# The three low-rank inputs of an RWKV-7 time-mix: shifting the input, or mixing the weights

## The chip, the cores and the metric

One core of one Trainium2 chip runs the whole program. The metric is the device time of one execution in microseconds (us). The engines are TensorE (PE; PEld is its weight load), VectorE (DVE), ScalarE (ACT), GpSimd (POOL) and SyncE (SP), which issues nearly all the transfers.

## What is computed

The program is a decoder trunk of two layers for 1024 tokens of 1024 channels, float32: an RWKV-7 time-mix with its MLP, then sliding-window attention with its MLP. The change is in the time-mix, in the inputs of its projections:

```python
xx = token_shift(h) - h                    # token_shift: the row before, zeros ahead of the first
xs = h[None] + xx[None] * mu[:, None, None, :]
r, k, v = jnp.einsum('nbtc,ncd->nbtd', xs[:3], w_rkv)
xv, xw, xa, xg = xs[2], xs[3], xs[4], xs[5]
w_log = -jax.nn.softplus(-(w0 + jnp.tanh(xw @ w1) @ w2)) - 0.5
a = jax.nn.sigmoid(a0 + (xa @ a1) @ a2)
g = jax.nn.sigmoid(xg @ g1) @ g2
```

Six inputs are made from h and its shifted copy. Three feed full matrices (r, k, v: 1024 x 1024), three feed low-rank ones: decay (w1, 64 columns), rate (a1, 64) and gate (g1, 160). Then come a recurrence over the tokens for 16 heads, a normalisation, the gate and an output matrix.

## The kernel before

**Precision.** A float32 product is made of three products in float32r: each operand is split into a high half (a cast on ScalarE, line 129) and a low half (a subtraction, line 130), and `mm3` adds high x high, high x low and low x high (lines 134 to 136). So every operand costs a cast and a subtraction ahead of PE. Weights arrive in a "wr" tile (5 buffers), are split into "wh" (4) and "wl" (3), and split inputs lie in "m2k" tiles (24 buffers). A few small products use plain float32, such as line 535, the sums of squares per head.

**Parts.** The projections run in three parts of 256, 256 and 512 tokens (`PARTS`), each a call of `project`. `channels` normalises and transposes x into h: tiles "b8" of 257 columns, with the token ahead in column 0. `steps` makes the differences of neighbouring tokens on GpSimd for the parts of 256. `shifted` makes one input i: for each of 8 tiles of 128 channels it mixes h and its neighbour with mu (line 353; lines 357 and 358 in the part of 512) and splits the result, on GpSimd's subtraction for the first 8, 4 and 0 tiles of a part (`POOLED`), else on VectorE's. `thin` multiplies such an input with a low-rank matrix; `lora_out` and `gate_out` are the second, wide product of the low-rank pairs. `values` makes v for a part, in one PSUM bank per 128 tokens, and `prod` one 128-channel group of r or k. The pools hold eight PSUM banks: four "big" for the projections and the MLP, two "sm" and two "sq" for the recurrence.

**Order.** In a part, the gate's second product of the part before (`left`) and the first thin input alternate for nine steps; then values; then the groups of r and k, after each of which a number of steps of the generator `small` is taken (`STEPS1`, `STEPS2`): the rest of the thin inputs, their second products, and the channels of the next part. Results go to HBM (dP, dG, dV). A part's groups of heads end with the inverse norms of k (lines 548 to 560): line 559 closes a group, and the recurrence reads its result in `prep` (600 to 602).

**The recurrence** takes units of 128 tokens and 8 heads, 16 in all, through `prep`, `inner`, `solve` (on GpSimd), `join`, `chunks` and `finish`. Its instructions have priority over the projections. Units 0 to 3 need part 0, units 4 to 7 part 1, units 8 to 15 part 2. After unit 7 the first half of the tokens goes on: `mixed` and `mix_out`, then the MLP of that half, beside units 8 to 15. A scheduler puts the instructions into an order for each engine by priority and by its own estimate of time when the program is built; every engine, and SP's queue of transfers, then works in that order.

## Time and profile before

| | |
|---|---|
| median of 3 runs | 2687.38 us (2681.1 to 2687.82) |
| profiled execution | 2683.85 us, its span 2682.1 us |
| mean granted clock of TensorE | 0.974 of full speed |
| busy: PE, PEld, DVE, ACT, POOL | 2549.6, 2066.2, 1688.0, 1289.1, 616.9 us |
| instructions: PE, DVE, ACT, POOL | 15226, 3204, 2670, 1213 |
| DMA | 349.62 MB, mean 130 GB/s |

The profile shows one execution. Busy time is the union of an engine's instructions; matmuls overlap each other, so the sum of their durations is more than PE's busy time. A granted clock of 1 is TensorE at 2.4 GHz, 0.5 at 1.2 GHz, and a mean lies between. A wait names the instruction that came last before the waiting one could start. The projections fill the first 666 us, the recurrence runs from 104 to about 1230 us, the MLPs and the attention from about 770 us to the end.

### The profile page before, as it was taken

The page shows a single profiled execution, that of the slowest core. Times are in us where ns is not written, and L with a number is a line of the kernel's source. Part 1 is how long each engine was busy: PE and PEld are TensorE (multiplying, and loading weights), DVE is VectorE, ACT ScalarE, POOL GpSimd, SP SyncE. Part 2 cuts the span into 40 slices and gives each one's busy share as a digit, 9 for nine tenths or more (in the row PEclk, how much of TensorE's full clock was granted, in tenths as well). Part 3 has the DMA queues.
Part 4 walks back from the last instruction along what each step waited for, and adds up shares of the span by engine and source line. Part 5 has one row for each costly group of instructions (what it writes and reads, how often), then busy time and mean ns, then how long its engine had stood idle before and what let it go on. Part 6 is the DMA issues. An engine that isn't in the chain of part 4 may idle for free.

```text
span 2682.1 us, 43180 instructions
## 1 busy us (share of the span) xinstructions
PE 2549.6 (95%) x15226; PEld 2066.2 (77%) x15226; DVE 1688.0 (63%) x3204; ACT 1289.1 (48%) x2670; POOL 616.9 (23%) x1213
## 2 busy tenths in 40 slices
PE   7978988998889999999999999999999999999999
PEld 5867766765767777778888888888888888888887
DVE  8678788665766666545467876445899544444444
ACT  5555566455444434334455555334666433434342
POOL 6276643741464444410010000001000000000000
PEclk9988989999889999999999999999999999999999
DMA  5756644654634444333434444342446332423332
GB/s 178 203 171 171 181 115 121 181 145 148 178 101 117 121 117 117 109 103 119 142 94 150 123 129 146 92 154 90 136 142 204 114 102 91 125 91 102 98 98 96
DMA packets 440633, 349.62 MB, mean 130 GB/s; under 512 B 97105, under 2 KB 360417, under 8 KB 440417
## 3 DMA queue, kind: packets, MB, share of 16 engines
q1 hardware_dynamic: 423008, 344.77, 42.5%
q10 hardware_dynamic: 17408, 2.10, 0.5%
q8 instruction: 120, 1.97, 0.3%
q14 instruction: 97, 0.79, 0.1%
HBM read 280.71 MB, written 57.67 MB: 126 GB/s over the span
## 4 chain that ended last, share of the span: by engine, by line
PE 54%; DVE 2%; DMA 0%; ACT 0%; issue 0%; POOL 0%; DVEq 0%; ACTq 0%; POOLq 0%
PE big L134 17%; PE big L135 17%; PE big L136 17%; PE sm L134 1%; PE sm L135 0%; PE sm L136 0%; PE sq L956 0%; PE sq L957 0%; PE big L252 0%; DVE sc L962 0%; DVE wl L130 0%; DVE m2k L260 0%; PE sq L933 0%; DMA wr<-in_b_wq 0%; DVE b L1038 0%; DVE st L966 0%
## 5 line engine op out<-in xcount | busy, mean ns | idle before, releaser
L129 ACT CAST wh<-wr 128x512 fp32r<-128x512 f32 x741 | 458.2, 620 | 872.4 <-PE big L136 457.5
L130 DVE TENSOR_TENSOR wl<-wr,wh 128x512 fp32r<-128x512 f32 x741 | 529.4, 718 | 485.5 <-issue 226.0
L135 PE MATMUL big<-wl,m2k 128*128 128x512 f32 (+1 forms) x1472 | 580.6, 395 | 7.2 <-DVE wl L130 5.4
L134 PE MATMUL big<-m2k,wh 128*128 128x512 f32 (+3 forms) x1528 | 576.4, 380 | 9.8 <-ACT m2k L129 4.8
L136 PE MATMUL big<-m2k,wl 128*128 128x512 f32 (+2 forms) x1528 | 571.3, 376 | 7.4 <-DVE wl L130 7.3
L135 PE MATMUL big<-m2k,wh 128*128 128x512 f32 (+2 forms) x1528 | 571.1, 375 | 7.3 <-POOL m2k L130 4.2
L136 PE MATMUL big<-wh,m2k 128*128 128x512 f32 (+1 forms) x1472 | 567.5, 392 | 2.8 <-POOL m2k L130 2.8
L134 PE MATMUL big<-wh,m2k 128*128 128x512 f32 (+1 forms) x1472 | 515.9, 395 | 9.8 <-ACT m2k L129 7.5
L134 PEld LDWEIGHTS big<-m2k,wh 128*128 128x128 f32 (+1 forms) x1528 | 290.3, 190 | 70.8 <-ACT m2k L129 6.9
L136 PEld LDWEIGHTS big<-m2k,wl 128*128 128x128 f32 (+1 forms) x1528 | 290.8, 191 | 59.6 <-DVE wl L130 10.1
L134 PEld LDWEIGHTS big<-wh,m2k 128*128 128x128 f32 x1472 | 281.3, 192 | 71.1 <-ACT m2k L129 9.2
L135 PEld LDWEIGHTS big<-m2k,wh 128*128 128x128 f32 (+1 forms) x1528 | 290.6, 190 | 58.5 <-POOL m2k L130 6.7
L135 PEld LDWEIGHTS big<-wl,m2k 128*128 128x128 f32 x1472 | 282.1, 192 | 69.2 <-DVE wl L130 10.4
L136 PEld LDWEIGHTS big<-wh,m2k 128*128 128x128 f32 x1472 | 281.2, 191 | 59.3 <-POOL m2k L130 3.3
L680 POOL TENSOR_TENSOR tmp<-Xs,TT 128x60 f32<-128x60 f32 (+24 forms) x496 | 193.6, 390 | 142.0 <-DMA Xs<-dXs 105.4
L130 DVE TENSOR_TENSOR m2k<-relu,m2k 128x512 fp32r<-128x512 f32 (+1 forms) x200 | 137.0, 687 | 122.7 <-ACT m2k L129 122.0
L682 POOL TENSOR_TENSOR TT<-TT,tmp 128x60 f32<-128x60 f32 (+24 forms) x496 | 199.1, 401 | 37.8
L129 ACT CAST m2k<-relu 128x512 fp32r<-128x512 f32 (+1 forms) x272 | 146.4, 544 | 46.3 <-DVE relu L353 33.8
L322 DVE TENSOR_TENSOR b<-b,big 128x512 f32<-128x512 f32 x192 | 124.8, 681 | 10.2 <-PE big L136 9.7
L223 POOL TENSOR_TENSOR ss<-ss,mhalf 128x4 f32<-128x4 f32 (+1 forms) x10 | 8.9, 888 | 488.7 <-DVE ss L222 488.7
L223 POOL TENSOR_TENSOR qn<-qn,mhalf 128x8 f32<-128x8 f32 x16 | 26.7, 1671 | 399.3 <-DVE qn L222 346.0
L314 ACT ACTIVATE relu<-relu 128x512 f32<-128x512 f32 x128 | 80.8, 632 | 3.5
(229 smaller groups left out, 3089.7 us busy)
## 6 DMA issues: line engine op xcount, KB each, us to landing
wr<-in_mlp_w SPq DMA_DIRECT2D x512, 256.0 KB, 2.7
wr<-in_a_w_rkv SPq DMA_DIRECT2D x144, 256.0 KB, 3.1
ld<-dP SPq DMA_DIRECT2D x16, 1024.0 KB, 7.7
dS<-sc SPq DMA_DIRECT2D x28, 512.0 KB, 2.9
row<-dS SPq DMA_DIRECT2D x112, 128.0 KB, 2.8
dP<-stg SPq DMA_DIRECT2D x64, 128.0 KB, 2.8
AR<-RA SPq DMA_DIRECT2D x32, 256.0 KB, 4.5
Xs<-dXs SPq DMA_DIRECT2D x64, 128.0 KB, 2.7
```

The lines of the kernel that those rows point to most:

```text
L129: self.nc.scalar.copy(hi, src)
L130: (engine or self.nc.vector).tensor_tensor(lo, src, hi.bitcast(F32), ALU.subtract)
L134: mm(ps, ah, bh, start=start, stop=False)
L135: mm(ps, ah, bl, start=False, stop=False)
L136: mm(ps, al, bh, start=False, stop=stop)
L223: nc.gpsimd.tensor_tensor(dst, dst, self.mhalf[:, :n], ALU.pow)
L314: nc.scalar.activation(r, r, AF.Square)
L322: nc.vector.tensor_tensor(v, v, ps[tt], ALU.add)
L680: nc.gpsimd.tensor_tensor(v, Xs[:, k:k + 1, k + 1:].broadcast_to([P, m, n]), TT[:, 0:m, k:k + 1].broadcast_to([P, m, n]), ALU.mult)
L682: nc.gpsimd.tensor_tensor(TT[:, 0:m, k + 1:], TT[:, 0:m, k + 1:], v, ALU.add)
```

## The change

The token shift is linear, so h + (shifted - h) * mu times W equals h times ((1 - mu) W) plus the shifted h times (mu W). The three low-rank matrices (64 + 64 + 160 = 288 columns) are multiplied by (1 - mu) and by mu once, in part 0, by GpSimd; 256 of the mixed columns are split into halves and stored to HBM (dL), and read back in parts 1 and 2. h itself is split once, 257 columns of it, and each pair of tiles is streamed twice through PE, the second time moved by one column (`small_in`). The last 32 columns of the gate are kept in plain float32 (`last`): their products are written to four groups of 32 PSUM partitions, two of the eight channel tiles in each, and `gate_in` adds the four. All three inputs' first products are now done in the nine steps ahead of values; three PSUM banks are held meanwhile. "m2k" tiles become 516 columns wide, and the step counts are shorter.

```diff
--- before.py
+++ after.py
@@ -41,6 +41,9 @@
 PARTS = [(0, 256), (256, 256), (512, 512)]
 PART = [(i, t) for i, (_, n) in enumerate(PARTS) for t in range(0, n, TB)]
 
+MIXED = [(3, 0, 2), (4, 2, 2), (5, 4, 5)]
+UNITS = 9
+
 M2K = 24
 WR = 5
 WH = 4
@@ -55,8 +58,8 @@
 ORDER2 = 'cispfj'
 POOLED = (8, 4, 0)
 
-STEPS1 = (0, 2, 2, 2, 2, 2, 2, 2, 2, 3, 3, 3, 3, 4, 4, 4)
-STEPS2 = (2, 2, 2, 2, 2, 2, 2, 3, 3, 3, 3, 3, 3, 3, 3, 3)
+STEPS1 = (0, 1, 1, 1, 1, 1, 1, 1, 1, 1, 1, 2, 2, 2, 2, 2)
+STEPS2 = (1, 1, 1, 1, 1, 2, 2, 2, 2, 2, 2, 2, 2, 2, 2, 2)
 
 PACE0 = 0.6
 PACE1 = 1
@@ -111,7 +114,10 @@
         return self.sq.tile([P, 512], F32, tag="sq", name=self.nm("sq"))
 
     def m2k(self):
-        return self.t(self.mp, "m2k", [P, 512], F32R, M2K)
+        return self.m2k_wide()[:, :512]
+
+    def m2k_wide(self):
+        return self.t(self.mp, "m2k", [P, 516], F32R, M2K)
 
     def parts(self, n):
 
@@ -204,6 +210,11 @@
                                     channel_multiplier=0)
         self.mhalf = cp.tile([P, NT * H], F32, name="mhalf")
         nc.vector.memset(self.mhalf, -0.5)
+
+        self.mixes = cp.tile([P, KT, 2, UNITS], F32, name="mixes")
+        for i, u0, n in MIXED:
+            for j, v in enumerate((self.vec2[:, i * KT:(i + 1) * KT], self.vec[:, m0 + i * KT:m0 + (i + 1) * KT])):
+                nc.vector.tensor_copy(self.mixes[:, :, j, u0:u0 + n], v.unsqueeze(2).broadcast_to([P, KT, n]))
         self.hlast = cp.tile([P, KT], F32, name="hlast")
         nc.vector.memset(self.hlast, 0.0)
 
@@ -330,6 +341,8 @@
         self.dP = [part(f"dP{g}_", lambda m: [P, 4, GP, m]) for g in range(NG)]
         self.dG = [part(f"dG{g}_", lambda m: [P, GP, m]) for g in range(NG)]
         self.dV = part("dV", lambda m: [m, C])
+        self.dL = [d(f"dL{k}", [2, P, 512]) for k in range(KT)]
+        self.dL3 = d("dL3", [P, KT, 2, 32])
         self.dZ = [d(f"dZ{i}", [P, KT, TH]) for i in range(2)]
         self.dX = [d(f"dX{i}", [TH, C]) for i in range(2)]
 
@@ -360,17 +373,67 @@
             self.split(hi, lo, a, nc.gpsimd if k < POOLED[self.pt] else None)
             yield hi, lo
 
-    def thin(self, hT, i, n, W, outs):
-
-        w = W.shape[-1]
-        m = min(512 // w, KT)
-        for k, (xh, xl) in enumerate(self.shifted(hT, i, n)):
-            if k % m == 0:
-                wh, wl = self.weight(W[k * P:min(k + m, KT) * P].rearrange("(k p) c -> p k c", p=P), [P, min(m, KT - k), w])
-            for ps, c0 in outs:
-                c = slice(c0, c0 + ps.shape[0])
-                self.mm3(ps, wh[:, k % m, c], wl[:, k % m, c], xh, xl, k == 0, k == KT - 1)
-            yield
+    def small_weights(self, pt):
+
+
+        nc, I = self.nc, self.I
+        last = self.t(self.mp, "wr", [P, KT, 2, 32], F32, WR)
+        if pt:
+            nc.sync.dma_start(last, self.dL3)
+        for k in range(KT):
+            hi, lo = self.t(self.mp, "wh", [P, 512], F32R, WH), self.t(self.mp, "wl", [P, 512], F32R, WL)
+            if pt:
+                for j, w in enumerate((hi, lo)):
+                    nc.sync.dma_start(w.bitcast(F32), self.dL[k][j])
+            else:
+                raw = self.t(self.mp, "wr", [P, UNITS * 32], F32, WR)
+                c = 0
+                for W in (I['a_w1'], I['a_a1'], I['a_g1']):
+                    nc.sync.dma_start(raw[:, c:c + W.shape[-1]], W[0, k * P:(k + 1) * P])
+                    c += W.shape[-1]
+                mixed = self.t(self.rp, "bk", [P, 2, UNITS, 32])
+                nc.gpsimd.tensor_tensor(mixed, raw.rearrange("p (u c) -> p u c", c=32).unsqueeze(1).broadcast_to([P, 2, UNITS, 32]),
+                                        self.mixes[:, k].unsqueeze(3).broadcast_to([P, 2, UNITS, 32]), ALU.mult)
+                v = lambda x: x.rearrange("p (j u c) -> p j u c", j=2, c=32)
+                nc.scalar.copy(v(hi), mixed[:, :, 0:8])
+                nc.vector.tensor_tensor(v(lo), mixed[:, :, 0:8], v(hi).bitcast(F32), ALU.subtract)
+                nc.gpsimd.tensor_copy(last[:, k], mixed[:, :, 8])
+                for j, w in enumerate((hi, lo)):
+                    nc.sync.dma_start(self.dL[k][j], w.bitcast(F32))
+            yield hi, lo, last
+        if not pt:
+            nc.sync.dma_start(self.dL3, last)
+
+    def small_in(self, hT, pt):
+
+        nc = self.nc
+        n = PARTS[pt][1]
+        self.inner_u = pd, pg, p3 = [self.bank()[:, :n] for _ in range(3)]
+        for k, (wh, wl, last) in enumerate(self.small_weights(pt)):
+            if n > 256:
+                hi, lo = self.m2k_wide()[:, :n + 1], self.m2k_wide()[:, :n + 1]
+            else:
+                m = self.m2k_wide()
+                hi, lo = m[:, :n + 1], m[:, 258:259 + n]
+            for j, h in enumerate(hT):
+                src = h[:, k, int(j > 0):]
+                c = slice(j * 256 + int(j > 0), (j + 1) * 256 + 1)
+                self.split(hi[:, c], lo[:, c], src)
+            for j in range(2):
+                s = slice(1 - j, 1 - j + n)
+                for i, ps in enumerate((pd, pg)):
+                    c = slice((2 * j + i) * P, (2 * j + i + 1) * P)
+                    self.mm3(ps, wh[:, c], wl[:, c], hi[:, s], lo[:, s], k == 0 and j == 0, k == KT - 1 and j == 1)
+            if k < KT - 1:
+                yield
+
+        for i, h in enumerate(hT):
+            for k in range(0, KT, 4):
+                for j in range(2):
+                    for q in range(4):
+                        nc.tensor.matmul(p3[32 * q:32 * q + 32, i * 256:(i + 1) * 256], last[:, k + q, j],
+                                         h[:, k + q, 1 - j:257 - j], start=k == 0 and j == 0, stop=k == KT - 4 and j == 1)
+        yield
 
     def lora_out(self, W2, u, off, dst, pt):
 
@@ -397,12 +460,15 @@
             nc.sync.dma_start(self.dP[o // GP][pt][:, dst, o % GP], e)
             yield
 
-    def gate_in(self, hT, pt):
-
-        nc, I = self.nc, self.I
+    def gate_in(self, pt):
+
+        nc = self.nc
         n = PARTS[pt][1]
-        p1, p2 = self.bank()[:, :n], self.bank()[:32, :n]
-        yield from self.thin(hT, 5, n, I['a_g1'][0], ((p1, 0), (p2, P)))
+        _, p1, p3 = self.inner_u
+        p2 = self.stg()[:32, :n]
+        nc.scalar.copy(p2, p3[0:32])
+        for q in range(1, 4):
+            nc.vector.tensor_tensor(p2, p2, p3[32 * q:32 * q + 32], ALU.add)
         uh, ul = self.parts(n)
         us = self.m2k()[:, :n]
         for ps, m in ((p1, P), (p2, 32)):
@@ -489,25 +555,25 @@
             for _ in range(m):
                 next(g, None)
 
-        def lora(W1, i, f, W2, off, dst):
-            ps = self.bank()[:64, :n]
-            yield from self.thin(hT, i, n, W1, ((ps, 0),))
-            u = self.t(self.mp, "relu", [P, 512], F32, RELU)[:64, :n]
-            nc.scalar.activation(u, ps, f)
-            yield from self.lora_out(W2, u, off, dst, pt)
-
         self.pt = pt
         self.steps(hT, n)
 
         groups = [range(KT)] if n > 256 else [range(GP), range(GP, KT)]
         steps = iter(STEPS1 if n > 256 else STEPS2)
-        decay = lora(I['a_w1'][0], 3, AF.Tanh, I['a_w2'][0], 6, 2)
-        rate = lora(I['a_a1'][0], 4, AF.Copy, I['a_a2'][0], 7, 3)
-        first = KT + 1 + len(groups[0])
-        small = chain(islice(decay, first), islice(rate, first), decay, rate, self.gate_in(hT, pt))
+        start = self.small_in(hT, pt)
         for _ in range(KT + 1):
             step(left)
-            step(small)
+            step(start)
+        us = []
+        for r0, f in ((0, AF.Tanh), (64, AF.Copy)):
+            us.append(self.t(self.mp, "relu", [P, 512], F32, RELU)[:64, :n])
+            nc.scalar.activation(us[-1], self.inner_u[0][r0:r0 + 64], f)
+        decay = self.lora_out(I['a_w2'][0], us[0], 6, 2, pt)
+        rate = self.lora_out(I['a_a2'][0], us[1], 7, 3, pt)
+        next(decay)
+        next(rate)
+        self.gate_in(pt)
+        small = chain(islice(decay, len(groups[0])), islice(rate, len(groups[0])), decay, rate)
         self.values(list(self.shifted(hT, 2, n)), pt)
         nxt = []
         if pt + 1 < len(PARTS):
```

## Rows read from the trace of the kernel before

**Rows 1.** The page, part 1: busy us, share of the span, instructions.

```profile
...
PE 2549.6 (95%) x15226; PEld 2066.2 (77%) x15226; DVE 1688.0 (63%) x3204; ACT 1289.1 (48%) x2670; POOL 616.9 (23%) x1213
...
```

**Rows 2.** Windows by stage: length, busy us per engine (instructions), granted clock, DMA share, GB/s.

```profile
...
0.00:16.70 16.70, 4.84 (x19) 3.28 (x19) 10.31 (x40) 9.18 (x18) 8.89 (x23) 1.00 0.70 225
...
0.00:155.00 155.00, 125.98 (x730) 101.94 (x731) 110.30 (x193) 89.67 (x203) 75.44 (x109) 0.96 0.61 185
155.00:364.00 209.00, 180.85 (x1693) 149.23 (x1692) 163.63 (x321) 118.38 (x281) 133.76 (x265) 0.89 0.59 166
364.00:666.00 302.00, 271.89 (x2117) 197.99 (x2118) 216.34 (x437) 171.30 (x363) 120.78 (x269) 0.95 0.49 146
666.00:804.00 138.00, 118.82 (x800) 95.92 (x799) 91.00 (x174) 58.01 (x113) 74.42 (x158) 0.85 0.50 141
804.00:2682.00 1878.00, 1852.07 (x9891) 1521.15 (x9889) 1106.78 (x2083) 851.75 (x1713) 212.52 (x414) 1.00 0.39 119
...
```

**Rows 3.** Timeline of PE and DVE, 664 to 760 us: start, duration, instruction.

```profile
...
664.50 0.68 PE L766 MATMUL sq<-RT,SV 64*64 64x64 f32 x16
...
666.36 0.23 DVE L559 TENSOR_SCALAR ssk<-big 128x64 f32<-128x64 f32 x1
...
758.88 0.69 PE L743 MATMUL sq<-SV,AR 128*64 128x64 f32 x16
...
```

**Rows 4.** PE's waits, 16 to 666 us: total us, times, longest.

```profile
...
PE big L134 <- ACT m2k L129: 12.3, 5, 4.9
PE big L136 <- DVE wl L130: 7.3, 6, 2.7
PE big L135 <- DVE wl L130: 5.4, 8, 1.2
...
PE big L135 <- POOL m2k L130: 4.2, 3, 1.9
...
```

**Rows 5.** DVE groups in 0:155, 155:364, 364:666: busy, mean ns, idle before.

```profile
...
L353 DVE SCALAR_TENSOR_TENSOR relu<-m2k,vec,b 128x256 f32<-128x256 f32 x52 | 37.4, 756 | 0.7 <-POOL m2k L130 0.6
...
L353 DVE SCALAR_TENSOR_TENSOR relu<-m2k,vec,b 128x256 f32<-128x256 f32 x44 | 22.6, 529 | 5.2 <-POOL m2k L130 4.9
L130 DVE TENSOR_TENSOR m2k<-relu,m2k 128x256 fp32r<-128x256 f32 x24 | 13.3, 559 | 2.7 <-ACT m2k L129 2.5
...
L358 DVE SCALAR_TENSOR_TENSOR relu<-b,vec,relu 128x256 f32<-128x256 f32 x90 | 41.0, 490 | 9.6 <-ACT relu L357 9.4
L130 DVE TENSOR_TENSOR m2k<-relu,m2k 128x512 fp32r<-128x512 f32 x48 | 33.6, 707 | 1.2 <-ACT m2k L129 1.1
...
```

**Rows 6.** ACT groups: the first row in 0:155, the others in 364:666.

```profile
...
L129 ACT CAST m2k<-relu 128x256 fp32r<-128x256 f32 x52 | 20.7, 407 | 20.1 <-DVE relu L353 20.0
...
L357 ACT ACTIVATE relu<-b,vec 128x256 f32<-128x256 f32 x90 | 40.6, 505 | 18.2 <-DVE m2k L130 18.1
L129 ACT CAST m2k<-relu 128x512 fp32r<-128x512 f32 x47 | 28.7, 619 | 8.6 <-DVE relu L358 8.3
...
```

**Rows 7.** POOL groups in 0:155.

```profile
...
L130 POOL TENSOR_TENSOR m2k<-relu,m2k 128x256 fp32r<-128x256 f32 x50 | 45.6, 933 | 50.2 <-ACT m2k L129 29.5 <-PE big L535 12.9 <-PE big L136 7.8
L344 POOL TENSOR_TENSOR m2k<-b 128x512 f32<-128x512 f32 x8 | 9.1, 1155 | 5.7 <-ACT b L475 5.7
...
```

**Rows 8.** Timeline of PE, at 80 and at 206 us.

```profile
...
79.96 0.61 PE L535 MATMUL big<-relu,ind 128*16 128x256 f32 x2
80.50 0.39 PE L134 MATMUL big<-m2k,wh 128*128 128x256 f32 x1
...
206.00 0.69 PE L743 MATMUL sq<-SV,AR 128*64 128x64 f32 x16
206.62 0.33 PE L665 MATMUL sm<-ident,bk 128*128 128x128 f32 x1
...
```

**Rows 9.** Waits of SP's queue, 0 to 666 us.

```profile
...
SPq L269 <- DVE wl L130: 146.5, 71, 13.7
...
```

**Rows 10.** The page, part 6: DMA issues, KB each, us to landing.

```profile
...
wr<-in_a_w_rkv SPq DMA_DIRECT2D x144, 256.0 KB, 3.1
...
```

## The prediction, made before the change was run

> **What bounds the kernel now.** I read the page first: TensorE (PE) is busy for 2549.6 of 2682.1 us [rows 1]. That says "bound by PE", but as a mean over stages. So next I cut the span into stages with the table of windows [rows 2]; the cuts are where VectorE's L559, the last small step of each group of heads, closes a part of the projections, the last of them at 666.36 us [rows 3]. After 804 us PE is busy for 1852 of 1878 us at the full clock: nothing but less PE work helps there. The idle time lies before: 155.0 - 126.0 = 29.0 us in part 0 (11.9 of it in the first 16.7 us, before the first product), 28.2 in part 1, 30.1 in part 2, and 19.2 between 666 and 804. The granted clock is 0.96, 0.89, 0.95 and 0.85 there, between the two levels of 1.2 and 2.4 GHz; against a full clock that is 6 + 23 + 15 + 21 = 65 us of stretch. So 72 us of idle time and 44 us of lower clock stand before 666 us, and this is all that a change in the projections can win.
>
> What ends the idle time is in PE's list of waits from 16 to 666 us [rows 4]: 12.3 us on ScalarE's high halves of the shifted inputs (line 129), 4.2 us on GpSimd's low halves (130) and some 6 us in two smaller rows of the same kind, and 7.3 and 5.4 us on VectorE's low halves of weights. About 35 us hang on preparing operands, the rest on the steps of the recurrence. VectorE is busy for 78% of part 1 and 72% of part 2 [rows 2], so operands queue up behind it.
>
> **The change, part by part.** *Removed on VectorE, ScalarE and GpSimd.* Three of the six inputs need no shift and split: 24 tiles per part. Part 0: 24 scalar_tensor_tensor of 0.756 us on VectorE [rows 5], 24 casts of 0.407 us on ScalarE [rows 6], 24 subtractions of 0.933 us on GpSimd [rows 7]. Part 1: 24 of 0.529 us and 12 subtractions of 0.559 us on VectorE [rows 5], 12 on GpSimd. Part 2: 48 of 0.490 us and 24 of 0.707 us on VectorE, and on ScalarE 48 of 0.505 us and 24 of 0.619 us [rows 5, 6]. Five weight splits per part go too (about 0.7 us on VectorE and 0.62 us on ScalarE each, as for the other tiles of 512 columns).
>
> *Added there.* h is split once: 8 tiles of 257 columns in parts 0 and 1, 16 in part 2, each about 0.5 us on VectorE (a little under the mean of 0.559 us for 256 columns, which holds some long ones) and 0.41 us on ScalarE [rows 5, 6]. Part 0 alone folds the weights: 8 GpSimd products of 576 elements, 1.3 us each from the 1.155 us for 512 [rows 7], 8 small copies, and 8 splits. Three additions, one copy and six small constants complete it. The net on VectorE is about -10, -18 and -35 us in parts 0, 1 and 2; on ScalarE -4, -9 and -35; on GpSimd -10, -11 and 0.
>
> *PE, the wide products.* Before: 24 + 24 + 48 = 96 products per part, of 64, 64 and 128 or 32 weight columns. After: 8 x 2 x 2 x 3 = 96, all with 128 columns and the same streamed length. I cost this at nothing.
>
> *PE, the last 32 gate columns.* These are new: 16 plain float32 products of 256 columns for each 256 tokens. One such product in the trace is two records: L535 starts at 79.96 us and the next product at 80.50 us, so 0.54 us [rows 8]. 4 x 16 x 0.54 = 35 us if they run one after another, 9 us if the four 32-column groups run side by side. The nearest row is L743, whose 16 records alternate between two halves of the output: 0.62 us in all, where one after another a quarter of 0.27 us each would make 1.08 us [rows 8]. Two groups so give 0.57 of the serial time; I take 10 us, near the low end, and keep 9 and 35.
>
> The Trainium skill (TensorE: Matmul & The Clock Gate, section "Measured speedup vs the span model") gives 2.38 times for three column tiles; worked out from that the products would take some 12 to 15 us, an estimate of that page and not a term here. The trace agrees that halves overlap; no row here shows four groups.
>
> *The front of part 0.* Each of the 8 weight tiles goes through one buffer ("bk", single): product 1.3 us, then cast 0.62 us and subtraction 0.7 us, so about 3 us with the hand-overs, 24 us in all, from about 12 us on. Meanwhile three of the four "big" PSUM banks are held, so the value products, which fill 27 to 58 us now, cannot start. But all three inputs' products are done then, and not only those of the decay. Queues that this passes: 24 loads and 16 stores of 256 KB more on SP in the first 40 us, 4.2 MB of stores in a part whose DMA share is 0.61 at 185 GB/s [rows 2]. I take +5 us; ends 0 and 15.
>
> *Loads in parts 1 and 2.* Sixteen loads of 256 KB take the place of the splits; one lands in 3.1 us [rows 10], and they need a free "wl" buffer, of which there are three, where one k takes PE 12 products. SP is in order and already waits 146.5 us for weight buffers in this stage [rows 9]; behind it wait the recurrence's loads. The cover is gate_out of the part before and the recurrence. With the cover gone: 8 x 1.7 us = 14 us in part 1. I take nothing. For the hand-over of the three banks I take 1 us per part, 3 us.
>
> *What comes back.* Of the 35 us of operand waits, half of the 22 us for shifted inputs (three of six) and 4 of the weight waits: 15 us. Of the other 37 us of idle time some 5, as VectorE's load falls by 9 to 16%. Together 20 of 72 us; the same share of the 44 us of lower clock is 12. Between 666 and 804 us the first chunk of unit 8 starts only at 758.88 us, though unit 7's last product starts at 664.50 us [rows 3]: its preparation needs the norms of part 2, which L559 gives at 666.36 us. If part 2 ends before unit 7 does, this stage has more to run; I take 8 of its 40 us. Ends of the whole return: 10 and 75 us.
>
> *The sum.* -15 - 5 - 12 - 8 + 10 + 5 + 3 = -22 us. The profiled execution took 2683.85 us (span 2682.1 and 1.75 around it): 2662 us. The median of the runs, 2687.38, is 3.5 us above that execution.
>
> **The rivals.** *The recurrence keeps its pace.* mix_out of the first half waits for unit 7, and unit 7 ends within 2 us of part 2 [rows 3]. If its chain is paced by its own hops, parts that end sooner leave PE with less to run beside it; only the earlier preparation of unit 8 pays, and some of that goes to the added products. 2680 us. For it: the chain is the first thing after 666 us that everything needs. Against it: its steps queue on the same VectorE, which is relieved most.
>
> *PE stays the bound, and the narrow products run one after another* (the side that is slower). Price 35 us on PE, in the projections, with 8 us for the front and the banks and 20 us returned: +23, 2707 us. It decides once a record costs over 0.25 us: then 128 of them eat the 32 us returned before 666 us. For it: PE is at 95% and gets more work. Against it: L743's overlap [rows 8]. The Trainium skill (Perfetto Trace Analysis, section "Identifying the Most-Contended Engine") says to optimize the engine with the highest occupancy first; by that rule this change, which relieves the others and loads PE, could only cost. The windows speak against the rule for this stage, where PE idles 10 to 19%.
>
> *The change does not free the engines' queues:* loads into the three "wl" buffers replace splits, SP blocks at them and holds up the recurrence's transfers. 14 us in part 1 and little in part 2: 2662 + 14 = 2676 us.
>
> **How the numbers follow.** Forecast 0.53, pace of the recurrence 0.20, PE-bound and serial 0.17, loads 0.10. The likeliest case gives 2662 us. Its own range, from the ends of the returns and of the front, is 2630 to 2685. For 8 in 10 I take in the recurrence and the load case whole and part of the slow one: 2632 to 2702. A measurement of this kernel can tell about 0.3%, or 8 us, from no change. Faster by more: 0.50 of the forecast, 0.09, 0.01 and 0.06 of the others, 0.66. The same: 0.03 + 0.10 + 0.05 + 0.03 = 0.21. Slower: 0.13.
>
> **What would show it.** Right: the closing L559 of part 2 well before 666 us, VectorE's busy time in the projections down by about 60 us, the waits of line 134 on ScalarE about halved, the narrow products taking under 3 us per 256 tokens, unit 8's first chunk well before 758 us. Wrong: narrow records 0.2 us or more apart; PE idle before 50 us with the value products late; unit 7 ending where it did; SP's waits for "wl" grown.

## The result: 1.0% slower, and the profile after

The changed kernel took 2710.98 us (median of 4 runs, 2705.5 to 2714.21), the kernel before 2684.39 us beside it (4 runs, 2681.1 to 2687.82): a ratio of 1.0103, 95% interval [1.0088, 1.0119]. The forecast was 2662 us with a range of 2632 to 2702: the wrong sign, and outside the range. The profiled execution took 2710.56 us, its span is 2708.8 us, 26.7 us more than before.

The change moved lines of the code: 134 to 136 are now 140 to 142, 129 and 130 are 135 and 136, 559 is 625, 743 is 809, 766 is 832. The narrow products are line 434, the folds 395 (GpSimd), 398 (ScalarE) and 399 (VectorE).

The page of the kernel after, busy time, beside [rows 1]:

```profile
PE 2586.9 (95%) x15354; PEld 2072.4 (77%) x15354; DVE 1630.8 (60%) x3112; ACT 1251.4 (46%) x2578; POOL 588.1 (22%) x1193
```

The relief came near the count: VectorE 57 us less, ScalarE 38, GpSimd 29 (63, 48 and 21 by the prediction). PE is busy for 37.3 us more, with only 128 records more. The windows by stage of the kernel after, with the columns of [rows 2], say where:

```profile
0.00:155.00 155.00, 123.68 (x725) 99.16 (x726) 96.29 (x187) 84.11 (x188) 56.19 (x73) 0.92 0.67 203
155.00:364.00 209.00, 181.44 (x1644) 150.43 (x1643) 142.22 (x286) 108.50 (x255) 127.26 (x279) 0.89 0.65 182
364.00:666.00 302.00, 276.44 (x2200) 205.90 (x2198) 190.04 (x375) 148.72 (x311) 118.40 (x270) 0.94 0.56 163
666.00:804.00 138.00, 124.29 (x907) 98.18 (x907) 93.07 (x182) 58.27 (x114) 73.93 (x157) 0.86 0.50 139
804.00:2709.00 1905.00, 1881.04 (x9886) 1518.70 (x9884) 1109.23 (x2086) 851.75 (x1713) 212.32 (x414) 1.00 0.39 117
```

Up to 804 us the two kernels are nearly level: PE idles 98 us in place of 106, the clock is a little lower in the first 155 us, and 9886 records are left, 9891 before. The time is lost behind that. From there to the end the 9886 records need 1881 us of PE, where the 9891 needed 1852 [rows 2], at the same full clock, in code that the change does not touch. The timeline of the kernel after gives the same picture:

```profile
668.12 0.22 DVE L625 TENSOR_SCALAR ssk<-big 128x64 f32<-128x64 f32 x1
...
677.33 0.68 PE L832 MATMUL sq<-RT,SV 64*64 64x64 f32 x16
...
761.52 0.69 PE L809 MATMUL sq<-SV,AR 128*64 128x64 f32 x16
```

Part 2 closes at 668.12 us (666.36 before), unit 7's last product starts at 677.33 (664.50), unit 8's first chunk at 761.52 (758.88) [rows 3]: 2 to 3 us of the 26.7 are lost by then. The loss must show in a stretch of the last MLP where PE never stands still. First the window of 2300 to 2600 us of the kernel before, then that of the kernel after:

```profile
2300.00:2600.00 300.00, 299.49 (x1333) 247.40 (x1332) 130.36 (x199) 117.80 (x195) 0.00 (x0) 1.00 0.33 102
```

```profile
2300.00:2600.00 300.00, 299.52 (x1305) 242.07 (x1304) 124.41 (x190) 118.98 (x197) 0.00 (x0) 1.00 0.32 100
```

PE is busy for 299.5 us in both, at clock 1.00, but gets 28 records fewer done, 2.1%. Consecutive products of 128x512 start 226.7 ns apart before (nearly all 225 to 228) and 232 ns apart after (nearly all 224 to 240). PE's busy time cannot show this: it is full either way. The weight loads show it, 247.4 us against 242.1, 2.2%. The Trainium skill (Perfetto Trace Analysis, section "Identifying the Most-Contended Engine") says that the busy share of matmuls does not tell how near TensorE is to its limit, and that the load of weights does; this row and this stretch agree.

What could slow an unchanged product? The wide tile. The change makes each of the 24 "m2k" buffers 516 columns wide, 2064 bytes, and in the built program they lie 2080 bytes apart: the streamed operands, and all weights behind them, lie elsewhere than before.

### The profile page after: what moved, and what is told of

It is laid out like the page before. It is cut to its first block, busy times and chain, and to the rows that moved or that the text cites. A ratio compares the mean times of both kernels' runs of the same rounds, so it can differ in the third digit from the quotient of the medians.

```text
span 2708.8 us, 43352 instructions
## 1 busy us (share of the span) xinstructions
PE 2586.9 (95%) x15354; PEld 2072.4 (77%) x15354; DVE 1630.8 (60%) x3112; ACT 1251.4 (46%) x2578; POOL 588.1 (22%) x1193
## 4 chain that ended last, share of the span: by engine, by line
PE 55%; DVE 1%; DMA 0%; ACT 0%; issue 0%; SPq 0%; DVEq 0%; ACTq 0%
PE big L140 17%; PE big L141 17%; PE big L142 17%; PE sm L140 1%; PE sm L142 1%; PE sm L141 1%; PE sq L1022 0%; PE sq L1023 0%; PE big L263 0%; DVE sc L1028 0%; PE sq L999 0%; DVE m2k L271 0%; DMA wr<-in_b_wq 0%; DVE b L1104 0%; DVE wl L136 0%; ACT wh L285 0%
## 5 line engine op out<-in xcount | busy, mean ns | idle before, releaser
L135 ACT CAST wh<-wr 128x512 fp32r<-128x512 f32 x726 | 448.5, 620 | 928.0 <-PE big L142 468.9
L136 DVE TENSOR_TENSOR wl<-wr,wh 128x512 fp32r<-128x512 f32 x726 | 514.2, 712 | 531.9 <-PE big L142 185.8
L140 PE MATMUL big<-m2k,wh 128*128 128x512 f32 (+1 forms) x1528 | 581.9, 382 | 9.3 <-DMA wh<-dL 2.9
L142 PE MATMUL big<-m2k,wl 128*128 128x512 f32 (+1 forms) x1528 | 574.2, 379 | 2.0 <-DVE wl L136 1.2
L141 PE MATMUL big<-m2k,wh 128*128 128x512 f32 (+1 forms) x1528 | 573.3, 376 | 0.1
L140 PEld LDWEIGHTS big<-m2k,wh 128*128 128x128 f32 x1528 | 294.6, 193 | 72.7 <-DMA wh<-dL 3.5
L142 PEld LDWEIGHTS big<-m2k,wl 128*128 128x128 f32 x1528 | 292.7, 193 | 59.1 <-DVE wl L136 2.1
L141 PEld LDWEIGHTS big<-m2k,wh 128*128 128x128 f32 x1528 | 294.7, 193 | 52.6 <-issue 1.0
L746 POOL TENSOR_TENSOR tmp<-Xs,TT 128x60 f32<-128x60 f32 (+24 forms) x496 | 187.5, 378 | 131.8 <-DMA Xs<-dXs 94.7
L136 DVE TENSOR_TENSOR m2k<-relu,m2k 128x512 fp32r<-128x512 f32 (+1 forms) x164 | 113.9, 697 | 121.9 <-ACT m2k L135 120.4
L135 ACT CAST m2k<-relu 128x512 fp32r<-128x512 f32 (+1 forms) x200 | 113.2, 568 | 33.2 <-DVE relu L366 28.0
L234 POOL TENSOR_TENSOR qn<-qn,mhalf 128x8 f32<-128x8 f32 x16 | 26.7, 1671 | 406.3 <-DVE qn L233 352.2
```

The costliest lines, as they stand in the source:

```text
L135: self.nc.scalar.copy(hi, src)
L136: (engine or self.nc.vector).tensor_tensor(lo, src, hi.bitcast(F32), ALU.subtract)
L140: mm(ps, ah, bh, start=start, stop=False)
L141: mm(ps, ah, bl, start=False, stop=False)
L142: mm(ps, al, bh, start=False, stop=stop)
L234: nc.gpsimd.tensor_tensor(dst, dst, self.mhalf[:, :n], ALU.pow)
```

## The experiments

All ratios are against the kernel before on the same chip at the same time. Spacings are the differences between the starts of consecutive 128x512 products in the trace.

**e1: the kernel before, with m2k tiles 516 wide.** Nothing else; every engine's queue is the same, instruction for instruction.

```diff
-        return self.t(self.mp, "m2k", [P, 512], F32R, M2K)
+        return self.t(self.mp, "m2k", [P, 516], F32R, M2K)[:, :512]
```

> The kernel before with one edit: each m2k tile is allocated 516 columns wide and only 512 are used; every engine's instructions stand in the same order. Theory A (where the tiles lie in SBUF sets the pace of the products): back-to-back products of 512 columns start about 232 ns apart instead of 227, a full 300 us stretch of the last MLP holds about 1305 products instead of 1333, and the time is 1.009 to 1.017 of before. Theory B (the time lost after 1300 us comes from another order of the work, more transfers or the clock): ratio 1.000 within 0.002, spacing 227 ns.

Measured: 2713.47 us, ratio 1.0106 [1.0089, 1.0123]. The span is 2706.6 us, the spacing 232 ns, and the window of e1 reads as that of the kernel after:

```profile
2300.00:2600.00 300.00, 299.51 (x1306) 242.29 (x1305) 125.13 (x191) 119.77 (x198) 0.00 (x0) 1.00 0.33 100
```

So the width of a buffer, with no other part of the change, costs what the whole change costs.

**e2: the change, tiles 528 wide** (a multiple of 64 bytes, same queues as the change).

```diff
-        return self.t(self.mp, "m2k", [P, 516], F32R, M2K)
+        return self.t(self.mp, "m2k", [P, 528], F32R, M2K)
```

> The changed kernel with m2k tiles of 528 columns, so that they lie at multiples of 64 bytes instead of 16 (32 with the padding), same order of instructions. If a start at a multiple of 64 bytes is what counts: spacing back to 227 ns, some 38 us less than the changed kernel, ratio to before 0.993 to 0.998. If it is that the two operands of a product start at the same place within 2048 bytes: spacing stays at 230 to 233 ns, ratio 1.007 to 1.013. Theory B: as the changed kernel, 1.010.

Measured: 2714.51 us, ratio 1.0113 [1.0097, 1.0129], spacing 231.7 ns. Alignment to 64 bytes does not mend it.

**e3: the change, tiles 512 wide.** In part 2 the 513 columns of h's halves go into the wide "row" tiles, in parts 0 and 1 each half has an m2k tile of its own.

```diff
-        return self.m2k_wide()[:, :512]
+        return self.t(self.mp, "m2k", [P, 512], F32R, M2K)
...
-        return self.t(self.mp, "m2k", [P, 516], F32R, M2K)
+        return self.t(self.mp, "row", [P, C], F32R, ROWS)
...
-                m = self.m2k_wide()
-                hi, lo = m[:, :n + 1], m[:, 258:259 + n]
+                hi, lo = self.m2k()[:, :n + 1], self.m2k()[:, :n + 1]
```

> The changed kernel with m2k tiles of 512 columns again; the split of h takes two m2k tiles in the parts of 256 and two row tiles in the part of 512. Theory A: spacing 227 ns, the last MLP as before; the rest of the change then shows alone, ratio to before 0.990 to 0.998 (some 38 us less than the changed kernel). Theory B: still 1.008 to 1.012.

Measured: 2691.78 us, ratio 1.0016 [1.0003, 1.0029]; span 2683.5 us, spacing 226.7 ns. The window of e3:

```profile
2300.00:2600.00 300.00, 299.48 (x1333) 247.34 (x1333) 130.15 (x199) 118.19 (x196) 0.00 (x0) 1.00 0.34 103
```

The two parts add up within the noise: 24.5 us of span for the width (e1) and 1.4 for the rest (e3) against 26.7 for the change; 1.06% and 0.16% against 1.03% by the ratios. The 1.4 us are two single executions, and e3's was the fastest of its ten: by the medians the rest costs 4.2 us. Either way it was forecast at -22. The queues of e3 are in another order than those of the change, so e3 alone could owe its time to that; the finding rests on e1, e4 and e13, whose queues are those of the kernel before.

**e4: the kernel before, relu tiles 520 wide.** m2k stays where it was; the weights, which lie behind relu, move by 3 x 32 = 96 bytes. The queues are the same.

```diff
-                r = self.t(self.mp, "relu", [P, 512], F32, RELU)
+                r = self.t(self.mp, "relu", [P, 520], F32, RELU)[:, :512]
```

(and so in the three other places)

> The kernel before with the three relu tiles allocated 520 columns wide, 512 used, same order. m2k tiles stay where they were, 2048 bytes apart; the weight tiles wr, wh and wl all move by 96 bytes against them. If the place of a product's two operands relative to each other counts: spacing 230 to 234 ns, ratio 1.008 to 1.017. If only the m2k tiles' own stride counts: 227 ns and ratio 1.000 within 0.002. Theory B: 1.000.

Measured: 2722.68 us, ratio 1.0142 [1.0126, 1.0157], spacing 234 ns, the window of e4:

```profile
2300.00:2600.00 300.00, 299.52 (x1294) 240.34 (x1293) 127.16 (x194) 118.64 (x196) 0.00 (x0) 1.00 0.33 100
```

The m2k tiles are untouched here, so it is not their width. What counts is where the weights lie relative to the operand that streams.

**m1: that distance by itself.** No part of the model, only eighteen lines like this one, 96 products each, all over one tile (the first line is a second 0, 0, as a run-up, and not in the table):

```python
for i in range(96): mm(bank(i), w(i, 96), m(i, 0), start=i % 8 == 0, stop=i % 8 == 7)
```

`w(i, x)` is a weight block that begins x bytes past a multiple of 512 in that tile, `m(i, x)` a streamed block x bytes past a multiple of 2048.

> Nothing of the reference is computed here: eighteen blocks of 96 products 128x128 by 128x512, back to back, each block with its weights and its moving operand begun at set distances (bytes past a multiple of 512 for the weights, of 2048 for the moving operand). Theory: what counts is where a product's two operands lie relative to each other. Then the blocks with equal distances (0 and 0, 320 and 320, 256 and 256) start a product every 226 to 228 ns and most of those with unequal ones (0 and 32 to 448, 320 and 0, 128 and 256) every 230 to 236 ns. Rival 1, the alignment of each operand by itself: 320 and 320 is slow as well. Rival 2, the place does not count and the slower pace came from the engines that work beside TensorE: all blocks are at 226 to 228 ns.

Measured, from the starts:

| streamed, weights at (bytes) | mean spacing, ns |
|---|---|
| 0, 0; 0, 256; 256, 256; 320, 320 | 226.7, 226.8, 226.8, 227.1 |
| 0, 192; 0, 448; 320, 0 | 228.9 each |
| 0, 4; 0, 128; 0, 384 | 232.4, 232.5, 232.3 |
| 0, 16; 0, 32; 0, 64; 0, 288; 128, 256 | 233.3 each |
| 0, 96; 0, 352 | 234.3 each |

The groups of lines in the profile of m1 (line 41 is 0, 0; 46 is 0, 96; 49 is 0, 256; 54 is 320, 320; 55 is 320, 0):

```profile
L46 PE MATMUL acc<-src 128*128 128x512 f32 x96 | 22.6, 396 | 0.0
...
L55 PE MATMUL acc<-src 128*128 128x512 f32 x96 | 22.1, 391 | 0.0
L54 PE MATMUL acc<-src 128*128 128x512 f32 x96 | 22.0, 389 | 0.0
L49 PE MATMUL acc<-src 128*128 128x512 f32 x96 | 21.9, 389 | 0.0
...
L41 PE MATMUL acc<-src 128*128 128x512 f32 x96 | 21.9, 389 | 0.0
```

Distances that leave the same remainder by 256 bytes give equal spacings: 0 and 256, 32 and 288, 96 and 352, 128 and 384, 192 and 448, and -320 with 192. The pair 128, 256 is off by a little: its distance is 128 too, and it takes 233.3 ns where 0, 128 takes 232.5. A whole multiple of 256 is the fast case, wherever the pair lies. Both rivals fall: 320, 320 is fast, and there are fast and slow blocks with nothing running beside TensorE.

In m1 all products of a block lie alike. In the change and in e1 tiles of all distances alternate, and there the pairs that lie right are not fast by themselves: with the addresses of the built programs, some 610 back-to-back products from about 1240 us on in the kernel after have a distance that is a multiple of 256 bytes, and they start 232.3 ns apart, some 530 in e1 230.0 ns. The pace of 226.7 ns was seen only where the products around lie right as well.

**e13: e4's edit with 576 columns in place of 520.** The weights move by 768 bytes, 3 x 256; the queues are again the same.

> The kernel before, with the three relu tiles 576 columns wide in place of 512 (520 cost 1.4%): weights now lie 768 bytes, a multiple of 256, further from the shifted inputs than before, in a kernel whose queues are the same instruction for instruction. Theory from the blocks of products (0 and 256 bytes: 226.8 ns; 32 to 128, 288 to 384: 232 to 234; 192 and 448: 228.9): only the distance modulo 256 bytes counts, so the products start every 227 ns and the time is that of before, 2683 to 2690 us (ratio 0.9985 to 1.0015). Rival, any move of the weights from the common place modulo 512 or 2048 costs: 230 ns or more and 1.006 to 1.014.

Measured: 2684.49 us against 2684.42, ratio 1.000 [0.9985, 1.0015], and the window of e13 has the records of the kernel before:

```profile
2300.00:2600.00 300.00, 299.49 (x1333) 247.38 (x1333) 129.83 (x198) 117.69 (x194) 0.00 (x0) 1.00 0.34 102
```

So a move of the weights by a multiple of 256 bytes costs nothing, and e4's move by 96 bytes does. (768 bytes is also what e1 moved the weights by, 24 x 32; there the m2k tiles themselves, 2080 bytes apart, no longer all lie a multiple of 256 bytes from the weights.)

**e7: the kernel before, attention's output tiles moved by 288 bytes** (a pad ahead of "oh" and "ol"), so that they too lie a multiple of 256 from their weights.

```diff
         self.v = self.t(self.ap, "v", [P, 2 * nv + 1, D], F32R)
+        nc.gpsimd.memset(t("pad", [P, 72]), 0.0)
```

> The kernel before, with a pad of 288 bytes ahead of the attention's output tiles, so that these begin at the same place modulo 2048 as the weights that they are multiplied with. Theory (relative placement): the 384 products of these tiles start every 227 ns in place of every 233 ns, the others stay at 227; the end comes 2 to 3 us earlier, 2684.5 to 2685.5 us (ratio 0.9989 to 0.9993). Rival, these products are slow for what runs beside them: 233 ns and no change.

Measured: 2683.80 us against 2685.49, ratio 0.9997 [0.9984, 1.001]. Groups of lines from 1600 us on, in the kernel before, with one of the same shape on top:

```profile
L135 PE MATMUL big<-m2k,wh 128*128 128x512 f32 x628 | 244.6, 390 | 0.0
L135 PE MATMUL big<-wl,oh 128*128 128x512 f32 x128 | 50.6, 396 | 0.0
L136 PE MATMUL big<-wh,ol 128*128 128x512 f32 x128 | 50.6, 395 | 0.0
L134 PE MATMUL big<-wh,oh 128*128 128x512 f32 x128 | 44.9, 395 | 0.0
```

and in e7:

```profile
L135 PE MATMUL big<-wl,oh 128*128 128x512 f32 x128 | 49.9, 390 | 0.0
L136 PE MATMUL big<-wh,ol 128*128 128x512 f32 x128 | 49.8, 389 | 0.0
L134 PE MATMUL big<-wh,oh 128*128 128x512 f32 x128 | 44.1, 389 | 0.0
```

Their spacing went from 233.3 to 226.7 ns, as expected; the 2 to 3 us that this gives are less than these runs can tell. The slow pace stood in the trace of before, in these 384 products: 395 ns a product, where the first row has 390.

The other question: why was the rest of the change worth +1.4 us (4.2 by the medians) and not -22? The runs for it are weaker: e5, e6, e9 and e12 have the queues in another order than e3, and e11 has them, but for PE's, in another order than the kernel before.

**e11: relief alone.** The kernel before, the three inputs' shifts and most of their splits left out, nothing added.

```diff
         for k in range(KT):
+            if i > 2:
+                if i == 3 or k == 0:
+                    hi, lo = self.parts(n)
+                    for j, h in enumerate(hT):
+                        c = slice(j * 256, j * 256 + 256)
+                        self.split(hi[:, c], lo[:, c], h[:, k, 1:])
+                yield hi, lo
+                continue
```

> The kernel before, with the relief of the change and none of its additions: the first of the three low-rank inputs is the split of h itself without a shift, the other two take the first pair of tiles again for every k (shifts and splits are left out, so these three inputs are not the model's). TensorE's instructions stay as they are. The forecast's terms for what comes back (15 us of operand waits, 5 of other idle time, 12 of lower clock, 8 between 666 and 804 us) give 2645 us (ratio 0.985). Rival, the recurrence and TensorE's own work set the end, and engines that are freed only move the waits: 2674 to 2684 us (ratio 0.9955 to 0.9995).

Measured: 2670.02 us, ratio 0.9944 [0.9923, 0.9964]; the span is 13.8 us shorter than before. Neither end: the relief is worth about 14 us (17 by the medians), a third of the 40 forecast or a little more, and slightly more than the rival's best. The windows of e11, with the columns of [rows 2]:

```profile
0.00:155.00 155.00, 125.43 (x748) 104.06 (x749) 98.19 (x183) 86.88 (x195) 56.05 (x88) 0.97 0.63 191
155.00:364.00 209.00, 181.57 (x1699) 149.35 (x1696) 150.03 (x301) 111.11 (x263) 120.83 (x250) 0.87 0.58 161
364.00:666.00 302.00, 281.56 (x2130) 207.06 (x2130) 189.44 (x379) 154.98 (x325) 131.74 (x270) 0.95 0.53 155
666.00:804.00 138.00, 125.21 (x943) 101.38 (x944) 102.33 (x193) 59.46 (x118) 74.71 (x174) 0.89 0.51 141
```

PE's idle time before 804 us is 90 us in place of 106, and the lower clock costs 62 us of stretch in place of 65. The waits of PE from 16 to 666 us in e11 show where the rest stayed:

```profile
PE big L134 <- ACT stg L458: 8.3, 2, 7.9
PE big L135 <- DVE wl L130: 6.8, 7, 1.6
PE big L134 <- ACT m2k L129: 5.9, 4, 2.6
PE big L563 <- ACT stg L557: 5.1, 3, 2.5
```

The wait on line 129 fell from 12.3 to 5.9 us [rows 4]; in its place stands one of 7.9 us on a free PSUM bank (line 458 empties it).

**e5: two buffers for the folds**, on e3.

```diff
-                mixed = self.t(self.rp, "bk", [P, 2, UNITS, 32])
+                mixed = self.t(self.rp, ("bk", "RA")[k % 2], [P, 2, UNITS, 32])
```

> The change with 512-column tiles, and the folded weights of part 0 made in two buffers in turn in place of one. Theory 1, TensorE's own work and idle add up to the end: the 8 us in which TensorE stands still at 38 to 46 us shrink by 3 to 8 us and the end moves by as much, 2684 to 2689 us beside a kernel before at 2687.5 (ratio 0.9985 to 1.0005). Theory 2, the recurrence sets when the first half ends, whatever the front does: the stall shrinks, the eighth unit of the recurrence still ends at 676 to 684 us, and the end stays within 2 us of 2692 (ratio 1.001 to 1.0025). If the folds' buffer is not what the products wait for, the stall stays at 7 to 9 us.

Measured: 2682.32 us against 2685.49, ratio 0.9991 [0.9977, 1.0006], span 2679.0 us. PE's stall ahead of the first value product shrank; in e3 it reads

```profile
46.98 0.80 PE L140 MATMUL big<-wh,m2k 128*128 128x512 f32 x1 [8.27 <-ACT m2k L135]
```

and in e5

```profile
43.33 0.50 PE L140 MATMUL big<-wh,m2k 128*128 128x512 f32 x1 [4.47 <-ACT m2k L135]
```

The stall fell by 3.8 us and the span by 4.5, the ratio by 0.25%: theory 1's numbers. But the second buffer also put all queues into another order, and no run separates the two.

**e12: no fold at all**, on e3 (the GpSimd product replaced by the raw weights).

```diff
-                mixed = self.t(self.rp, "bk", [P, 2, UNITS, 32])
-                nc.gpsimd.tensor_tensor(mixed, raw.rearrange("p (u c) -> p u c", c=32).unsqueeze(1).broadcast_to([P, 2, UNITS, 32]),
-                                        self.mixes[:, k].unsqueeze(3).broadcast_to([P, 2, UNITS, 32]), ALU.mult)
+                mixed = raw.rearrange("p (u c) -> p u c", c=32).unsqueeze(1).broadcast_to([P, 2, UNITS, 32])
```

> The change with 512-column tiles, and part 0's folded weights replaced by the raw ones, twice (the eight GpSimd products with the shift's coefficients and their one buffer are left out, so the three low-rank inputs see h and its shifted copy with the same weight). Casts, subtractions, stores and TensorE's instructions stay. Theory: relief of 14 us is taken back by 7 us of narrow products and 8 us of the front; then without the fold the stall of 8.3 us at 38 us falls to 0 to 4 us, part 2 closes 4 to 8 us earlier than the 671 us of the one with the fold, and the end is 2010 to 2016 us after that close: 2676 to 2681 us (ratio 0.9975 to 0.9995). Rival, the front is covered by what comes later: part 2 closes at 669 to 673 us and the ratio stays at 1.001 to 1.0025.

Measured: 2692.18 us, ratio 1.0017 [1.0005, 1.003]: a miss, and the rival's ratio (its close, 669 to 673 us, is missed by 1.3). It is that of e3 (1.0016), so nothing was gained by leaving the folds out. The stall is still 6.3 us. The value products start 5 us earlier than in e3 (41.73 and 46.98 us), part 2 closes 3.4 us earlier, at 667.7 us, and the end is no earlier.

**e6 and e9: the narrow products twice and three times**, on e3. (e9 has 3 in place of 2.)

```diff
-            for k in range(0, KT, 4):
+            for k in range(0, 2 * KT, 4):
```

> The change with 512-column tiles, and the narrow products of the ninth 32-column weight unit issued twice (that unit's sum comes out doubled). The 256 records added hold TensorE for 7 to 9 us by the 1.9 us that 32 of them took. Theory 1, TensorE's work adds up to the end: 2697 to 2702 us beside a kernel before at 2687.5 (ratio 1.0035 to 1.0055). Theory 2, the recurrence sets the pace to 804 us and covers them: 2690 to 2694 us (ratio 1.001 to 1.0025).

> The change with 512-column tiles, and the narrow products of the ninth weight unit issued three times (that unit's sum comes out threefold). Doubled they made the kernel faster by 15 us, with the queues in another order and a granted clock of 0.976 in place of 0.973. Theory 1, that gain came from the new order and the clock that went with it, not from the products: thrice gives another order again and lands anywhere between 2672 and 2702 us, with the records still at 1.9 us per 32, and the time follows the lower-clock stretches. Theory 2, work that keeps TensorE going where it would stand still raises the clock by itself: thrice is at least as fast as doubled, 2670 to 2678 us.

Measured: twice 2676.66 us against 2685.49, ratio 0.997 [0.9957, 0.9982]; three times 2699.34 us against 2687.21, ratio 1.0047 [1.0031, 1.0063]. (The expectation of e9 says that twice was faster by 15 us: that is its median beside e3's; the spans differ by 9.3.) Twice is a miss for both theories: 0.46% faster than e3 by the ratios. Three times is slower than e3 by 14.5 us of span, but by 8 us by the ratios (0.31%), which is 4 to 7 us for each 128 records. So theory 2 of e9 fell, and the added products are not what made e6 faster. What is left is another order of the queues: in e6 part 2 closes at 650.9 us and the clock is 1.00 from 804 to 1226 us, in e3 671.1 us and 0.98. That is argued, not shown, since no run changes the order alone. If it is so, an order is worth some 10 us, and it limits what a single edit of this kernel can be credited with.

Most of what sets these kernels apart stands at part 2's close (one execution of each):

| kernel | part 2 closes, us | span, us | span less close |
|---|---|---|---|
| before | 666.4 | 2682.1 | 2015.7 |
| e11, relief alone | 652.7 | 2668.3 | 2015.6 |
| e3, change with 512 columns | 671.1 | 2683.5 | 2012.4 |
| e5, and two fold buffers | 665.7 | 2679.0 | 2013.3 |
| e9, narrow three times | 684.8 | 2698.0 | 2013.2 |
| e10, e5 with e7's pad | 668.5 | 2678.7 | 2010.2 |
| e7, before with the pad | 669.4 | 2686.3 | 2016.9 |
| e13, before with relu 576 | 666.9 | 2686.8 | 2019.9 |
| e12, no fold | 667.7 | 2688.0 | 2020.3 |
| e6, narrow twice | 650.9 | 2674.2 | 2023.3 |
| after | 668.1 | 2708.8 | 2040.7 |
| e2, change with 528 columns | 676.6 | 2719.4 | 2042.8 |
| e1, before with 516 columns | 660.9 | 2706.6 | 2045.7 |
| e4, before with relu 520 | 667.9 | 2718.8 | 2050.9 |

Before, e7 and e13 have the same queues (e7 one small write more) and the fast pace in the long stretches, and they differ by 4.2 us in the last column: so much is the chance of one execution, and e12 lies no further off than e13. The kernels at the fast pace stand from 2010 to 2020 us, with e6 at 2023 and its unit 7 ending 27 us behind part 2; why is open. The four with misplaced tiles stand from 2041 to 2051 us.

**e10: e5 with e7's pad**, the version that the runs point to.

> The change with 512-column tiles, two buffers for the folds, and the attention's output tiles begun where the weights begin modulo 2048. If the two gains add, 3 us for the front (8 us of idle time fell to 4.5) and 2 to 3 us for 384 products at 227 in place of 233 ns: 2678 to 2681 us beside a kernel before at 2685.5 (ratio 0.997 to 0.9985). If the front's gain was the accident of another order of the queues, that order is kept here and only the 2 to 3 us of the products come on top of 0.9991, the same range; so a ratio above 0.9995 speaks against the price of the products.

Measured: 2682.21 us against 2687.21, ratio 0.9983 [0.9969, 0.9996], span 2678.7 us. It is faster than the kernel before by some 0.2%, by an interval that only just leaves 1 out, and by the two ratios 1.2% faster than the change as made.

## Why the prediction was wrong

**The step that failed** is "PE, the wide products": "I cost this at nothing". The count was right, 96 products per part with the same streamed length. What was not costed is the buffer that the moved stream needs: tiles of 516 columns shift operands against weights by amounts that are no multiple of 256 bytes, and the products that stream or load an m2k tile, some 7,800 records of 128x512 in the whole program, start 4 to 5 ns later on average where they stand back to back. e1 prices it at 24.5 us with the rest of the change absent, e3 takes it out, e13 shows that moving by a multiple of 256 bytes is free. This is half of the miss of 49 us (+26.7 us in place of -22), and it alone made the change clearly slower.

**The sum without it.** The other half is a second step that failed, the term "what comes back". The forecast for the rest was -22 us; e3 measured +1.4 (span) to +4.2 (medians). By its terms:

- *What comes back*, -40: the mechanism was right, the size was not. e11, which has the relief and none of the additions, gives -14: 16 us less idle time for some 28 forecast, 3 us of clock for the 12. In the kernel after, operand waits fell from about 35 us [rows 4] to 16 (8.2, 3.5, and three smaller ones of 4.4 together), but the change has new ones on its own weights (3.4 on the last columns, 2.9 on the loads from dL, two small ones), so some 12 us came back of the 15 forecast. PE's idle time before 804 us fell by 8 us only, because PE waits for the next thing. PE's waits from 16 to 666 us in the kernel after:

```profile
PE sm L683 <- DVE ld L678: 13.9, 2, 12.7
PE big L140 <- ACT m2k L135: 8.2, 1, 8.2
PE sq L809 <- DVE SV L828: 7.9, 2, 4.1
PE sq L771 <- DVE XT L766: 5.9, 4, 4.3
...
PE big L141 <- DVE wl L136: 3.5, 9, 1.2
PE big L434 <- POOL wr L400: 3.4, 4, 2.3
...
PE big L140 <- DMA wh<-dL: 2.9, 2, 2.6
```

  Three of the first four are steps of the recurrence. And the 12 us of lower clock did not come back: by the windows, 65 us of stretch before 804 us became 73 (0.92 of 155 us, 0.89 of 209, 0.94 of 302, 0.86 of 138). Between 666 and 804 us the condition of the 8 us was met: part 2 closed 9 us before unit 7's last product, where it closed 2 us behind it before, and PE's idle time there fell from 19.2 to 13.7 us. But that came of unit 7 ending 13 us later, not of part 2 ending sooner, and at 804 us the kernel was no further than before.
- *Narrow products*, +10: right in kind and near in size. Four groups of 32 columns run side by side; the timeline of the kernel after has the 32 records of 256 tokens in 1.9 us, 58 ns apart:

```profile
177.80 1.94 PE L434 MATMUL big<-b,wr 128*32 128x256 f32 x32
179.66 0.39 PE L140 MATMUL big<-m2k,wh 128*128 128x256 f32 x1
```

  That is 4 x 1.9 = 7.6 us of PE; e9's 4 to 7 us per 128 records at the end does not contradict it. The estimate from the Trainium skill (TensorE: Matmul & The Clock Gate, section "Measured speedup vs the span model"), 12 to 15 us, was too high for these.
- *The front*, +5: near, and probably too low. The fold's chain goes through one buffer as described, about 2.7 us a turn, and the value products come at 46.61 us, behind a stall of 8.21:

```profile
38.12 0.28 PE L142 MATMUL big<-m2k,wl 128*128 128x256 f32 x1
46.61 0.79 PE L140 MATMUL big<-wh,m2k 128*128 128x512 f32 x1 [8.21 <-ACT m2k L135]
```

  What the forecast missed is what the wait is for. The last fold is done before 38 us and the last low-rank product by 38.4. The value products wait for their own shifted inputs (the releaser is the cast of line 135 into an m2k tile), and ScalarE comes to these only after it has emptied the low-rank sums and split them (lines 469 to 482):

```profile
39.75 0.36 ACT L469 COPY stg<-big 32x256 f32<-32x256 f32 x1
...
45.74 0.40 ACT L482 CAST m2k<-stg 32x256 fp32r<-32x256 f32 x1
46.15 1.02 ACT L135 CAST m2k<-relu 128x256 fp32r<-128x256 f32 x3
```

  e12, without the folding product, still waits 6.3 us. The clock paid too: 0.88 of full speed from 17 to 58 us, 1.00 before.
- Relief of 14, narrow products of 7.6 and a stall of 8 leave about +2, and e3 measured +1.4 to +4.2. That the prices add up so is argued, not shown: they are from one trace or run each, with the queues in different orders, and e12 did not follow the sum.
- Two figures of the prediction do not come out of its own rows, without changing the forecast. The idle time from 16.7 to 666 us is 75 us and not 72 [rows 2]. And the ends of the returns and of the front give 2622 to 2702 us for the likeliest case, not 2630 to 2685.

**The rivals.** The slower one, PE as the bound with serial narrow products, came closest in time (2707 us), but by luck: the narrow products ran side by side. The rule of the Trainium skill (Perfetto Trace Analysis, section "Identifying the Most-Contended Engine") beside it, to optimize the most contended engine first, pointed the right way: PE's pace was what decided, though not through the work that the change adds. "The recurrence keeps its pace", 4 us under before, is nearest to e3, which lies 1 to 4 us over it: much of what was freed on other engines came back as waits on the recurrence's steps. Of the loads there is little to see: SP's wait on line 280 for "wl" buffers is 137.9 us, below the 146.5 of [rows 9], and PE waits 2.9 us for them.

**What was to show it.** VectorE's busy time before 666 us fell by 61.7 us (60 forecast), a narrow group takes 1.9 us (under 3): right. The waits on ScalarE's high halves fell by a third (12.3 to 8.2 us), not by half. The closing step of part 2 at 668.12 and unit 8 at 761.52 us failed. Of the signs of being wrong two came: the value products were late, with PE idle before 50 us, and unit 7 ended no sooner, but 13 us later. No sign looked at the pace of the products.

## What to carry to other kernels

Give the tiles that TensorE multiplies a size that is a multiple of 256 bytes per partition, and after every change of a buffer's width or of what is allocated ahead of weights, compare the spacing of back-to-back products in a stretch that the change does not touch. A busy share of 100% hides a loss of pace; the count of records in a fixed window shows it in one row. And work taken off engines that TensorE waits for returns a part of the waits only: price it by the next wait in line; here the relief returned a third of what was forecast from the list of waits and the clock.

## What the runs showed of the hardware

In a queue of 128x512 float32r products that all have their weights a whole multiple of 256 bytes from the streamed operand, one starts every 226.7 ns at the full clock (m1, and the long stretches of before, e3 and e13). At other distances it takes 228.9 to 234.3 ns, up to 3.4% more (m1). It is the distance and not either address, but for one pair that is 0.9 ns off, and pairs that lie right among others that do not are not fast (230.0 ns in e1, 232.3 in the kernel after). The profile books the extra time as busy. Why is not shown. In this kernel it moved the end by 1.0 to 1.4% through buffers 16 to 64 bytes wider.
